# Block products of four recurrence heads in one PSUM bank and one run

## The chip, the cores and the metric

The kernel runs on one core of a Trainium2 chip. The metric is the device time of one execution in microseconds (us), the median of several runs. A core has TensorE (PE; its weight loads are listed apart as PEld), VectorE (DVE), ScalarE (ACT), GpSimd (POOL) and SyncE (SP, which issues most DMAs). The profile comes from one further execution, recorded by the hardware profiler.

## The reference

Two layers of a hybrid decoder trunk for 512 tokens of width 1024. Each layer normalises its input, projects it, runs two groups of heads, and projects back with a residual. What matters here is the recurrence group (8 heads with 128 x 128 states):

```python
def hgrn2(q, f_logit, i, lb):
    qf = jax.nn.silu(q.astype(jnp.float32))
    logf = jnp.logaddexp(jnp.log(jnp.maximum(lb, LB_FLOOR)),
                         jnp.log1p(-lb) + jax.nn.log_sigmoid(f_logit.astype(jnp.float32)))
    k = -jnp.expm1(logf)
    ...
        scores = jnp.einsum('bhtd,bhsd,bhtsd->bhts', qch, kch, decay)
        o = jnp.einsum('bhts,bhsv->bhtv', scores, vch)
        o = o + jnp.einsum('bhtd,bhdv->bhtv', qch * jnp.exp(b), state)
...
def hybrid_layer(x, w_in, w_out, g_pre, g_post, lb, g_head, sinks):
    h = rms_norm(x, g_pre)
    proj = jnp.einsum('bsd,de->bse', h, w_in)
    q_h, f_h, i_h, z_h, q_a, k_a, v_a, z_a = jnp.split(proj, SPLIT_POINTS, axis=-1)
    o_h = hgrn2(q_h, f_h, i_h, lb)
    o_h = rms_norm(o_h, g_head).reshape(B, S, HG_WIDTH).astype(z_h.dtype) * jax.nn.silu(z_h)
    ...
    y = jnp.einsum('bse,ed->bsd', jnp.concatenate([o_h, o_a], axis=-1), w_out)
    return x + rms_norm(y, g_post)
```

## The kernel before

**Projections.** Every weight piece (128 x 512) is loaded by DMA into a tile `raw`, split by ACT into a rounded part `whi` (L181) and by DVE into the rest `wlo` (L182), and multiplied in three products per piece with the two parts of the activations `hhi` and `hlo` (L293). One call of `step()` issues three such matmuls. Two units of output (tiles `pj`, three PSUM banks) are in work at a time. The pieces are converted by a plan that counts steps and stays ahead of their use.

**Streams.** Attention and recurrence are generators that issue their own instructions and then yield a weight. `merge` interleaves them with the projection steps in proportion to these weights. So the weights that a generator yields set how many projection matmuls stand between two pieces of its work on PE. Instructions under `pin` keep the order in which the code issues them; the others are placed by a scheduler.

**Recurrence.** A head's masked score matrix `A` (128 x 128 for each of four token blocks) is built by levels: pairs of neighbouring tokens first (the base blocks), then blocks of 2, 4, 8, 16, 32 and 64. `prepare(a)` makes, for heads a and a + 1, the operands of the base products in the buffers `qb` and `kb` (L706 to L710) and the operands of the first level in `q` and `k` (L713 and L714). `spread` then issues 16 base products of 32 x 32 for a head (L688), four beside each other in the array by `tile_position`. As fp32 matmuls they count twice in the profile: 32 instructions MATMUL and as many weight loads for each head. The result of a head fills one bank, in the diagonal blocks only, and `keep_spread` copies it under a mask into `A` (L692). `hgrn(a)` takes four heads, a group, through the six levels: the products of a level (L744 for the first four levels, L750, L755) go into two of the three banks `sc`, in turn; then `q` and `k` are scaled for the next level (L762 on DVE, L763 on POOL), and DVE copies the products into `A` under a mask (L772). After that come the states and outputs, which use the two banks `ac`.

**The order around the change.** The base products of a group come in two runs on PE: those of the first two heads at the end of `prepare`, in two `sc` banks, and those of the other two at the start of `hgrn`, in the two `ac` banks. The buffers `qb` and `kb` of all heads come from the pool tag `b`, which holds two pairs, so the second two heads' operands follow the first two heads' products. After the second run `hgrn` yields 1.5, which becomes nine projection matmuls, and then the first level's products start. With two groups to a layer and two layers there are four groups.

Of the kernel before, what the change touches and what calls it, by code (L numbers as in the profile page):

```python
# [20 lines left out]
NT = SEQ // 128  # L21
# [49 lines left out]
def hybrid_kernel(ctx: ExitStack, tc: tile.TileContext, x, wkv, win, wout, g_pre, g_post, lbp, ghead, sinks,  # L71
                  gcol_c, cos_f, sin_f, cos_t, sin_t, masks_c, out):
    nc = tc.nc
    P = 128
# [9 lines left out]
    def pin(ins):  # L84
        return tc.keep_in_program_order(ins)
# [8 lines left out]
    def sc():  # L94
        sc_turn[0] += 1
        return sc_tiles[sc_turn[0] % SC]

    def ac():
        ac_turn[0] += 1
        return ac_tiles[ac_turn[0] % len(ac_tiles)]  # L100

    def tmp(tag, dt=F32, n=1):

        t = tp.tile([P, n, 512] if n > 1 else [P, 512], dt, tag=tag, name=tag, bufs=TB[tag])
        return t
# [25 lines left out]
    for l in range(1, DEPTH):  # L131
        i = plan_order.index((l, "kv"))
# [224 lines left out]
    def halves(tag):  # L357
        t = tmp(tag, n=2)
        return [t[:, 0], t[:, 1]]
# [77 lines left out]
    def layer(l, last):  # L437
# [240 lines left out]

        on = {}

        As, kbs, qbs, tots, quad = {}, {}, {}, {}, {}

        def spread(j, bank):

            for n in range(NT):
                for b in range(4):
                    c = slice(n * P + 32 * b, n * P + 32 * b + 32)
                    pin(nc.tensor.matmul(bank[32 * b:32 * b + 32, c], lhsT=kbs[j][:, c], rhs=qbs[j][:, c], start=True, stop=True,  # L688
                                         tile_position=(0, 32 * b)))

        def keep_spread(j, bank):
            nc.vector.copy_predicated(As[j].rearrange("p (n t) -> p n t", n=NT), bmask.unsqueeze(1).broadcast_to([P, NT, P]),  # L692
                                      bank.rearrange("p (n t) -> p n t", n=NT))

        def prepare(a):

            t = tmp("a", n=2)
            nc.gpsimd.memset(t, 0.0)
            blocks = lambda t, w: t.rearrange("p (b j) -> p b j", j=w)
            for j in range(a, a + 2):  # L700
                As[j] = t[:, j - a]
                f, k, q = quad[j] = fT.pop(j), kT.pop(j), qT.pop(j)
                f2, k2, q2 = (blocks(t, 2) for t in (f, k, q))
                qb, kb = halves("b")
                qb2, kb2 = blocks(qb, 2), blocks(kb, 2)
                nc.vector.reciprocal(kb2[:, :, 1], f2[:, :, 1])  # L706
                nc.scalar.copy(qb2[:, :, 0], q2[:, :, 0])
                nc.vector.tensor_tensor(qb2[:, :, 1], q2[:, :, 1], f2[:, :, 1], op=ALU.mult)
                nc.scalar.copy(kb2[:, :, 0], k2[:, :, 0])
                nc.vector.tensor_tensor(kb2[:, :, 1], kb2[:, :, 1], k2[:, :, 1], op=ALU.mult)  # L710
                qbs[j], kbs[j] = qb, kb

                nc.gpsimd.tensor_tensor(k2[:, :, 0], k2[:, :, 0], f2[:, :, 1], op=ALU.mult)  # L713
                nc.vector.tensor_tensor(q2, qb2, f2[:, :, 0].unsqueeze(2).broadcast_to([P, SEQ // 2, 2]), op=ALU.mult)  # L714
                nc.vector.tensor_tensor(f2[:, :, 0], f2[:, :, 0], f2[:, :, 1], op=ALU.mult)
                tots[j] = f2[:, :, 0]
                yield 3.5
            if a % 4 == 0:
                banks = [sc(), sc()]
                for i in range(2):  # L720
                    spread(a + i, banks[i])
                for i in range(2):
                    keep_spread(a + i, banks[i])

        def hgrn(a):
            hs = [(j, *quad.pop(a + j)) for j in range(4)]
            banks = [ac(), ac()]
            for i in range(2):
                spread(a + 2 + i, banks[i])
            for i in range(2):  # L730
                keep_spread(a + 2 + i, banks[i])
            yield 1.5
            for hh in (2, 4, 8, 16, 32, 64):
                nb = SEQ // (2 * hh)
                per, qu = nb // NT, nb // NT // 4
                Ls = [sc(), sc()]
                for j, f, k, q in hs:
                    L, i = Ls[j // 2], j % 2
                    qv = q.rearrange("p (b two j) -> p b two j", two=2, j=hh)
                    if hh <= 16:  # L740
                        for n in range(NT):
                            for b in range(4):
                                o_, blk, c = n * P + 32 * b, n * per + b * qu, 256 * i + n * 64 + 16 * b
                                pin(nc.tensor.matmul(L[32 * b:32 * b + 32, c:c + 16], lhsT=k[:, o_:o_ + 32],  # L744
                                                     rhs=qv[:, blk:blk + qu, 1, :], start=True, stop=True, tile_position=(0, 32 * b)))
                    elif hh == 32:
                        for n in range(NT):
                            for b in range(2):
                                o_, r_, c = n * P + 64 * b, 64 * b + 32 * (n % 2), 64 * i + n // 2 * 32
                                pin(nc.tensor.matmul(L[r_:r_ + 32, c:c + 32], lhsT=k[:, o_:o_ + 32],  # L750
                                                     rhs=q[:, o_ + 32:o_ + 64], start=True, stop=True, tile_position=(0, r_)))
                    else:
                        for n in range(NT):
                            o_, b, c = n * P, n % 2, 128 * i + n // 2 * 64
                            pin(nc.tensor.matmul(L[64 * b:64 * b + 64, c:c + 64], lhsT=k[:, o_:o_ + 64],  # L755
                                                 rhs=q[:, o_ + 64:o_ + 128], start=True, stop=True))
                for two in (hs[:2], hs[2:]):
                    for j, f, k, q in two:
                        qv = q.rearrange("p (b two j) -> p b two j", two=2, j=hh)
                        kv_ = k.rearrange("p (b two j) -> p b two j", two=2, j=hh)  # L760
                        tv = tots[a + j].rearrange("p (b two) -> p b two", two=2)
                        nc.vector.tensor_tensor(qv[:, :, 1, :], qv[:, :, 1, :], tv[:, :, 0].unsqueeze(2).broadcast_to([P, nb, hh]), op=ALU.mult)  # L762
                        nc.gpsimd.tensor_tensor(kv_[:, :, 0, :], kv_[:, :, 0, :], tv[:, :, 1].unsqueeze(2).broadcast_to([P, nb, hh]), op=ALU.mult)  # L763
                        t2 = sm.tile([P, nb], F32, tag=f"tot{hh}", name=f"tot{hh}", bufs=4)
                        nc.vector.tensor_tensor(t2, tv[:, :, 0], tv[:, :, 1], op=ALU.mult)
                        tots[a + j] = t2
                    for j, f, k, q in two:
                        A, L, i = As[a + j], Ls[j // 2], j % 2
                        if hh <= 16:
                            Av = A.rearrange("p (n b two j) -> p n b two j", n=NT, two=2, j=hh)[:, :, :, 1, :]  # L770
                            mv = lmask[hh].rearrange("p (b j) -> p b j", j=hh).unsqueeze(1).broadcast_to([P, NT, per, hh])
                            nc.vector.copy_predicated(Av, mv, L[:, 256 * i:256 * i + 256].rearrange("p (n b j) -> p n b j", n=NT, j=hh))  # L772
                        elif hh == 32:
                            Av = A.rearrange("p (m two t) -> p m two t", m=NT // 2, two=2)
                            for b in range(2):
                                for e in range(2):
                                    nc.scalar.copy(Av[64 * b:64 * b + 32, :, e, 64 * b + 32:64 * b + 64],
                                                   L[64 * b + 32 * e:64 * b + 32 * e + 32, 64 * i:64 * i + 64].rearrange("p (m t) -> p m t", m=NT // 2))
                        else:
                            Av = A.rearrange("p (m b t) -> p m b t", m=NT // 2, b=2)  # L780
                            for b in range(2):
                                nc.scalar.copy(Av[0:64, :, b, 64:128],
                                               L[64 * b:64 * b + 64, 128 * i:128 * i + 128].rearrange("p (m t) -> p m t", m=NT // 2))
                    yield 3.0

            kps = []
            for j, f, k, q in hs:
# [230 lines left out]
    m, n = head[0], head[1]  # L1018
# [43 lines left out]
    amask, bmask = masks[:, 0:128], masks[:, 128:256]  # L1062
# [40 lines left out]
    for run in [layer(l, l == DEPTH - 1) for l in range(DEPTH)]:  # L1103
        run()
# [60 lines left out]
```

## Time and profile before

| What | Value |
|---|---|
| Device time, median of 3 runs | 922.8 us (922.64 to 923.39) |
| Profiled execution: its span, first to last instruction | 921.4 us |
| Mean granted TensorE clock in it | 0.998 |
| HBM read, written | 86.93 MB, 12.58 MB |
| First run of base products of the first group | starts at 195.50 us |
| Second run; first level's products | 207.32; 210.30 us |

The page gives for each engine its busy time, share of the span and count of instructions. The chain is followed back from the last instruction: at each step to what released it. A group's row has line, engine, operation, output and input tiles, shape and count, then its busy time and the mean of one in ns, and the idle time ahead of it with what ended most of it. A row of the time line has start, duration, engine, line, operation and tiles, and in brackets the idle time before it with its releaser; rows of equal kind that follow each other are merged, with their count. A table by window has for each engine the busy time and in brackets how many instructions ran in the window. "issue" is a wait for nothing that the profile shows.

### The profile page before, as it was taken

The page shows a single profiled execution, that of the slowest core. Times are in us where ns is not written, and L with a number is a line of the kernel's source. Part 1 is how long each engine was busy: PE and PEld are TensorE (multiplying, and loading weights), DVE is VectorE, ACT ScalarE, POOL GpSimd, SP SyncE. Part 2 cuts the span into 40 slices and gives each one's busy share as a digit, 9 for nine tenths or more (in the row PEclk, how much of TensorE's full clock was granted, in tenths as well). Part 3 has the DMA queues.
Part 4 walks back from the last instruction along what each step waited for, and adds up shares of the span by engine and source line. Part 5 has one row for each costly group of instructions (what it writes and reads, how often), then busy time and mean ns, then how long its engine had stood idle before and what let it go on. Part 6 is the DMA issues. An engine that isn't in the chain of part 4 may idle for free.

```text
span 921.4 us, 19000 instructions
## 1 busy us (share of the span) xinstructions
PE 904.5 (98%) x7240; PEld 752.0 (82%) x7240; DVE 667.3 (72%) x1326; ACT 463.4 (50%) x1100; POOL 272.9 (30%) x292
## 2 busy tenths in 40 slices
PE   8999999999999999999989999999999999999996
PEld 7888887888888888888878878888788888888885
DVE  5967977869854896655786689876889449866556
ACT  6535767652755423534463366686446463245242
POOL 3325443304313142121332254450134022330102
PEclk9999999999999999999999999999999999999999
DMA  6684612333221432334356556222322323213413
GB/s 224 192 231 136 172 36 81 92 93 94 70 85 54 130 91 70 92 106 129 111 164 177 161 147 173 58 69 92 94 70 81 96 77 94 82 47 94 136 35 137
DMA packets 56570, 100.74 MB, mean 109 GB/s; under 512 B 6560, under 2 KB 9120, under 8 KB 56480
## 3 DMA queue, kind: packets, MB, share of 16 engines
q1 hardware_dynamic: 56192, 99.40, 36.6%
q8 instruction: 57, 0.93, 0.4%
q14 instruction: 33, 0.27, 0.1%
q10 hardware_dynamic: 288, 0.14, 0.1%
HBM read 86.93 MB, written 12.58 MB: 108 GB/s over the span
## 4 chain that ended last, share of the span: by engine, by line
PE 88%; DVE 6%; ACT 3%; issue 1%; POOL 1%; DMA 0%; POOLq 0%; DVEq 0%; ACTq 0%
PE pj L293 72%; PE sc L561 2%; PE sc L744 2%; PE ac L614 2%; PE ac L815 2%; DVE wlo L182 1%; PE ac L818 1%; PE ac L802 1%; PE sc L588 1%; ACT s L575 1%; PE sc L867 1%; PE sc L790 1%; POOL r L354 1%; DVE a L943 1%; PE sc L550 0%
## 5 line engine op out<-in xcount | busy, mean ns | idle before, releaser
L182 DVE TENSOR_TENSOR wlo<-raw,whi 128x512 fp32r<-128x512 f32 x249 | 182.9, 748 | 50.0 <-ACT whi L181 49.3
L181 ACT CAST whi<-raw 128x512 fp32r<-128x512 f32 x256 | 154.2, 620 | 106.0 <-PE pj L293 95.2
L293 PE MATMUL pj<-hhi,wlo 128*128 128x512 f32 x512 | 203.8, 398 | 0.0
L293 PE MATMUL pj<-hhi,whi 128*128 128x512 f32 x512 | 199.8, 390 | 0.0
L293 PE MATMUL pj<-hlo,whi 128*128 128x512 f32 x512 | 199.6, 390 | 0.0
L293 PE MATMUL pj<-whi,ops 128*128 128x512 f32 (+1 forms) x520 | 172.5, 394 | 0.0
L293 PEld LDWEIGHTS pj<-hhi,whi 128*128 128x128 f32 x512 | 96.1, 188 | 20.7
L293 PEld LDWEIGHTS pj<-whi,ops 128*128 128x128 f32 x520 | 97.2, 188 | 19.3
L293 PEld LDWEIGHTS pj<-hhi,wlo 128*128 128x128 f32 x512 | 96.1, 188 | 19.3
L293 PEld LDWEIGHTS pj<-hlo,whi 128*128 128x128 f32 x512 | 96.3, 188 | 18.6
L293 PE MATMUL pj<-whi,hlo 128*128 128x512 f32 x256 | 103.6, 405 | 0.0
L293 PE MATMUL pj<-wlo,ops 128*128 128x512 f32 (+1 forms) x260 | 100.8, 388 | 0.0
L293 PE MATMUL pj<-wlo,hhi 128*128 128x512 f32 x256 | 100.5, 392 | 0.3 <-DVE wlo L182 0.2
L293 PE MATMUL pj<-whi,hhi 128*128 128x512 f32 x256 | 100.3, 392 | 0.0
L763 POOL TENSOR_TENSOR k<-k,tot 128x256 f32<-128x256 f32 x80 | 64.2, 831 | 107.2 <-PE sc L744 57.7
L575 ACT ACTIVATE s<-sc,negm 128x128 f32<-128x128 f32 x128 | 45.5, 368 | 38.9 <-DVE negm L569 34.8
L762 DVE TENSOR_TENSOR q<-q,tot 128x256 f32<-128x256 f32 x80 | 48.8, 647 | 12.8 <-PE sc L750 7.0
L293 PEld LDWEIGHTS pj<-whi,hhi 128*128 128x128 f32 x256 | 48.1, 188 | 10.3
L293 PEld LDWEIGHTS pj<-wlo,ops 128*128 128x128 f32 x260 | 49.0, 188 | 8.8
L293 PEld LDWEIGHTS pj<-wlo,hhi 128*128 128x128 f32 x256 | 48.3, 189 | 9.1 <-DVE wlo L182 1.2
L293 PEld LDWEIGHTS pj<-whi,hlo 128*128 128x128 f32 x256 | 48.2, 188 | 8.0
L582 POOL TENSOR_TENSOR s<-s,sums 128x512 f32<-128x512 f32 x32 | 34.1, 1067 | 44.5 <-DVE sums L580 29.2
(188 smaller groups left out, 1416.2 us busy)
## 6 DMA issues: line engine op xcount, KB each, us to landing
raw<-in_win_dram SPq DMA_DIRECT2D x192, 256.0 KB, 2.7
raw<-in_wout_dram SPq DMA_DIRECT2D x64, 256.0 KB, 2.7
stack<-rot SPq DMA_DIRECT2D x16, 512.0 KB, 3.4
qs<-stack SPq DMA_DIRECT2D x32, 256.0 KB, 4.9
a<-in_x_dram SPq DMA_DIRECT2D x12, 256.0 KB, 3.0
raw<-in_wkv_dram SPq DMA_DIRECT2D x8, 256.0 KB, 4.2
x_mid<-a SPq DMA_DIRECT2D x8, 256.0 KB, 2.1
a<-x_mid SPq DMA_DIRECT2D x8, 256.0 KB, 3.2
```

What stands on the lines that cost most here:

```text
L181: keep(nc.scalar.copy(hi, v))
L182: keep((nc.gpsimd if i in on_pool and i % 2 else nc.vector).tensor_tensor(lo, v, hi.bitcast(F32), op=ALU.subtract))
L293: nc.tensor.matmul(u.o, lhsT=u.sta(k, u.w)[i], rhs=u.mov(k, u.w)[j], start=(n == 0), stop=(n == len(u.list) - 1))
L354: keep(nc.gpsimd.tensor_tensor(r, t, mhalf[:, 0:1], op=ALU.pow))
L561: pin(nc.tensor.matmul(S[:, h * 256:(h + 1) * 256], lhsT=q[:, 2 * hp_ + h, t_], rhs=kst[v][p][:, (n - 1) * P:(n + 1) * P], start=(h == 0 a ...
L575: nc.scalar.activation(pt[:, h * P:(h + 1) * P], cur[h], AF.Exp, bias=negm[:, h:h + 1], scale=SCALE, accum_out=sums[:, h:h + 1])
L582: nc.gpsimd.tensor_tensor(pv, pv, sums.unsqueeze(2).broadcast_to([P, 4, P]), op=ALU.mult)
L614: pin(nc.tensor.matmul(U, lhsT=vst[v][:, blk, :], rhs=d, start=(i == 0), stop=(i == len(terms) - 1)))
L744: pin(nc.tensor.matmul(L[32 * b:32 * b + 32, c:c + 16], lhsT=k[:, o_:o_ + 32], rhs=qv[:, blk:blk + qu, 1, :], start=True, stop=True, tile_ ...
L762: nc.vector.tensor_tensor(qv[:, :, 1, :], qv[:, :, 1, :], tv[:, :, 0].unsqueeze(2).broadcast_to([P, nb, hh]), op=ALU.mult)
L763: nc.gpsimd.tensor_tensor(kv_[:, :, 0, :], kv_[:, :, 0, :], tv[:, :, 1].unsqueeze(2).broadcast_to([P, nb, hh]), op=ALU.mult)
L815: pin(nc.tensor.matmul(O[:, c], lhsT=A[:, c], rhs=vs(j, n), start=(n == 0), stop=False))
```

## The change

The base products of all four heads of a group go into one `sc` bank, each block in 32 columns of its own, at the start of `hgrn`, directly ahead of the first level's products. `keep_spread` makes two copies of two heads each, spreading a block's 32 columns over the four places of a row under the same mask, and stands behind the first level's products. The first two heads' `qb` and `kb` stay in tag `b`; those of the other two come from the tags `s` and `u`. The yield of 1.5 ahead of the first level is gone, and the first level yields 4.5 instead of 3.0.

```diff
-        As, kbs, qbs, tots, quad = {}, {}, {}, {}, {}
-
-        def spread(j, bank):
-
-            for n in range(NT):
-                for b in range(4):
-                    c = slice(n * P + 32 * b, n * P + 32 * b + 32)
-                    pin(nc.tensor.matmul(bank[32 * b:32 * b + 32, c], lhsT=kbs[j][:, c], rhs=qbs[j][:, c], start=True, stop=True,
-                                         tile_position=(0, 32 * b)))
-
-        def keep_spread(j, bank):
-            nc.vector.copy_predicated(As[j].rearrange("p (n t) -> p n t", n=NT), bmask.unsqueeze(1).broadcast_to([P, NT, P]),
-                                      bank.rearrange("p (n t) -> p n t", n=NT))
+        As, pairs, kbs, qbs, tots, quad = {}, {}, {}, {}, {}, {}
+
+        def spread(a, bank):
+
+            for j in range(4):
+                for n in range(NT):
+                    for b in range(4):
+                        c, o_ = slice(n * P + 32 * b, n * P + 32 * b + 32), P * j + 32 * n
+                        pin(nc.tensor.matmul(bank[32 * b:32 * b + 32, o_:o_ + 32], lhsT=kbs[a + j][:, c], rhs=qbs[a + j][:, c],
+                                             start=True, stop=True, tile_position=(0, 32 * b)))
+
+        def keep_spread(a, bank):
+            for i in range(2):
+                nc.vector.copy_predicated(pairs[a + 2 * i].rearrange("p j (n b t) -> p (j n) b t", n=NT, b=4),
+                                          bmask.rearrange("p (b t) -> p b t", b=4).unsqueeze(1).broadcast_to([P, 2 * NT, 4, 32]),
+                                          bank[:, 256 * i:256 * i + 256].rearrange("p (m t) -> p m t", t=32).unsqueeze(2)
+                                          .broadcast_to([P, 2 * NT, 4, 32]))
...
+            pairs[a] = t
...
-                qb, kb = halves("b")
+                qb, kb = halves("b") if a % 4 == 0 else (tmp("s"), tmp("s" if j == a else "u"))
...
-            if a % 4 == 0:
-                banks = [sc(), sc()]
-                for i in range(2):
-                    spread(a + i, banks[i])
-                for i in range(2):
-                    keep_spread(a + i, banks[i])
...
-            banks = [ac(), ac()]
-            for i in range(2):
-                spread(a + 2 + i, banks[i])
-            for i in range(2):
-                keep_spread(a + 2 + i, banks[i])
-            yield 1.5
+            bank = sc()
+            spread(a, bank)
...
+                if hh == 2:
+                    keep_spread(a, bank)
...
-                    yield 3.0
+                    yield 4.5 if hh == 2 else 3.0
```

What stands where on PE in the first group, before (48 projection matmuls stand between the first two pieces, nine between the last two; of these the ones next to the products are shown):

```order
L688 MATMUL sc_79<-b 32x32 x16
L688 MATMUL sc_80<-b 32x32 x16
L293 MATMUL pj<-hhi,wlo 128x512
...
L293 MATMUL pj<-hhi,whi 128x512
L688 MATMUL ac_82<-b 32x32 x16
L688 MATMUL ac_81<-b 32x32 x16
L293 MATMUL pj<-hhi,wlo 128x512
...
L744 MATMUL sc_78<-q,k 32x16 x32
L744 MATMUL sc_79<-q,k 32x16 x32
L293 MATMUL pj<-hhi,wlo 128x512
```

The same place on PE in the changed kernel, where L689 is the base products and L739 the first four levels (a row's count is of fp32 matmuls, two instructions MATMUL each):

```order
L293 MATMUL pj<-hhi,whi 128x512
L689 MATMUL sc_79<-b 32x32 x32
L689 MATMUL sc_79<-s 32x32 x16
L689 MATMUL sc_79<-s,u 32x32 x16
L739 MATMUL sc_80<-q,k 32x16 x32
L739 MATMUL sc_78<-q,k 32x16 x32
L293 MATMUL pj<-hhi,wlo 128x512
```

The first run has moved back to the second, and the first level has moved up to it; the next level's products follow after 51 projection matmuls, 33 before. The other three groups read alike. On DVE at the same place, in the kernel before:

```order
L692 COPY_PREDICATED a<-masks,ac_82 128x512
L692 COPY_PREDICATED a<-masks,ac_81 128x512
...
L762 TENSOR_TENSOR q<-q,f 128x128x2
L846 TENSOR_TENSOR z_2395<-z_2394,oa 128x512
L762 TENSOR_TENSOR q<-q,f 128x128x2
L772 COPY_PREDICATED a<-masks,sc_78 128x128x2 x2
L848 TENSOR_TENSOR ops<-z_2395,ops 128x512
L182 TENSOR_TENSOR wlo<-raw,whi 128x512
```

And in the changed kernel (L694 is the masked copy of the base blocks, L759 the scaling of `q`, L769 the masked copy of a level, L843 a step of the output gate):

```order
L694 COPY_PREDICATED a<-masks,sc_79 128x1024 x2
L759 TENSOR_TENSOR q<-q,f 128x128x2 x2
L769 COPY_PREDICATED a<-masks,sc_80 128x128x2 x2
L759 TENSOR_TENSOR q<-q,f 128x128x2 x2
L843 TENSOR_TENSOR z_2469<-z_2468,oa 128x512
L182 TENSOR_TENSOR wlo<-raw,whi 128x512
```

The copies of all four heads now stand together, directly ahead of the first level's scaling and of the next `wlo`.

## The prediction

> **What bounds the kernel now.** I read the page first, then PE's time line around the runs that the change touches, then who waited for whom.
>
> ```profile
> PE 904.5 (98%) x7240; PEld 752.0 (82%) x7240; DVE 667.3 (72%) x1326; ACT 463.4 (50%) x1100; POOL 272.9 (30%) x292
> PE 88%; DVE 6%; ACT 3%; issue 1%; POOL 1%; DMA 0%; POOLq 0%; DVEq 0%; ACTq 0%
> q8 instruction: 57, 0.93, 0.4%
> ```
>
> PE is busy 98% of the span and 88% of the chain that ends last. Every other engine has slack. So each microsecond in PE's stream, gained or lost, moves the end by about as much, and the work is to price that stream. The third row (a DMA queue with its packets, MB and share) is needed below.
>
> ```profile
> 193.15 0.39 PE L293 MATMUL pj<-hhi,whi 128*128 128x512 f32 x1
> ...
> 195.19 0.39 PE L293 MATMUL pj<-hhi,whi 128*128 128x512 f32 x1
> 195.50 0.76 PE L688 MATMUL sc<-b 128*32 128x32 f32 x64
> 196.20 0.50 PE L293 MATMUL pj<-hhi,wlo 128*128 128x512 f32 x1
> 196.53 0.40 PE L293 MATMUL pj<-hlo,whi 128*128 128x512 f32 x1
> 196.77 0.40 PE L293 MATMUL pj<-hhi,whi 128*128 128x512 f32 x1
> ...
> 209.98 0.40 PE L293 MATMUL pj<-hhi,whi 128*128 128x512 f32 x1
> 210.30 1.35 PE L744 MATMUL sc<-q,k 128*32 128x16 f32 x128
> 211.58 0.50 PE L293 MATMUL pj<-hhi,wlo 128*128 128x512 f32 x1
> 211.92 0.39 PE L293 MATMUL pj<-hlo,whi 128*128 128x512 f32 x1
> 212.15 0.39 PE L293 MATMUL pj<-hhi,whi 128*128 128x512 f32 x1
> ```
>
> **A run's price.** From 193.15 to 195.19 nine projection matmuls start, 0.227 us apart. Around the first run of block products (64 instructions of the kind MATMUL) three such steps take 196.77 - 195.19 = 1.58 us instead of 0.68, so the run costs 0.90. Around the first run of level-2 products (128 of them) they take 2.17, so that run costs 1.49. The difference, 0.59 for 64 more, is 9.2 ns for each small matmul with its weight load. What is left of 0.90 is 0.31 us that a run costs for being a run: the time to go from wide tiles to narrow ones and back.
>
> **What the change removes from PE.** Each group of four heads had two runs of 64 and one of 128, 0.90 + 0.90 + 1.49 = 3.29 us. Now it has one run of 256: 0.31 + 256 x 0.0092 = 2.67. That is 0.62 per group and **2.5 us** for the four groups (four heads, two groups to a layer). The products themselves are as many and as large as before.
>
> **What the change adds to PE.** The level-2 run does not cost the same in all four groups:
>
> ```profile
> 319.74 1.56 PE L744 MATMUL sc<-q,k 128*32 128x16 f32 x128
> 664.93 1.66 PE L744 MATMUL sc<-q,k 128*32 128x16 f32 x128
> 774.57 1.37 PE L744 MATMUL sc<-q,k 128*32 128x16 f32 x128
> 664.93 1.13 PEld L744 LDWEIGHTS sc<-q,k 128*32 128x32 f32 x115 [0.36 <-issue]
> 666.28 0.21 PEld L744 LDWEIGHTS sc<-q,k 128*32 128x32 f32 x13 [0.23 <-issue]
> 319.70:320.85 1.15, 1.15 (x110) 1.10 (x109) 1.15 (x4) 0.91 (x2) 0.54 (x1) 1.00 0.79 280
> 320.85:666.20 345.35, 340.19 (x2406) 283.37 (x2396) 255.04 (x508) 174.25 (x434) 103.87 (x104) 1.00 0.39 117
> ```
>
> Two take 1.35 and 1.37, the other two 0.21 and 0.31 longer. In the longest, PE's weight loads stop after 115 of 128 and go on at 666.28, and the wait is put down to "issue": no engine or transfer that the profile knows was late. In the other the stop comes after 109 loads, near 320.8. The last row (a table by window; its second count is of weight loads) gives the distance: 2,396 loads, as many matmuls, and 72 semaphore instructions in the records between make 4,864 instructions, which is 19 x 256 exactly. And 256 is a known size: the queue of kind "instruction" in the first fence moved 57 packets of 0.93 MB / 57 = 16.3 KB, and PE's 7,240 matmuls and 7,240 loads make 254 instructions for each. So PE's code comes in blocks of 256 instructions, and both stops stand where one block ends. I read them as PE having used up a block before the next was there.
>
> How long does a block take to come? From the stop at 666.28 I go back 256 instructions: 115 loads and 115 matmuls, one semaphore, the nine projection matmuls with their loads (18), which leaves 7 in the tail of the run before:
>
> ```profile
> 661.95 0.65 PEld L688 LDWEIGHTS ac<-b 128*32 128x32 f32 x64 [0.35 <-issue]
> ```
>
> Its last load starts near 662.5 (0.65 us less one load of 0.11), and the block that was missing came 3.8 us later. The same count in the other group ends 19 instructions before the end of its run, near 317.2, and PE goes on near 320.9: 3.7 us. So a block seems to be asked for when PE enters the one before it, and is there some 3.75 us after. In the stream of projections 256 instructions last 128 x 0.227 = 29 us, so nothing is seen of it. In a run of small matmuls 256 instructions last 128 x 9.2 ns = 1.18 us.
>
> The joint run is 256 matmuls and 256 loads, 512 instructions without a pause: two ends of blocks lie in it, 1.18 us apart, and none of the three old runs held more than one. Counting the rows of the changed order from the known ends, the first lies about 146, 239, 251 and 88 instructions into the four joint runs, so the second, 256 further, lies inside each of them (at 507 of 512 in the third, where a few semaphores more or less don't matter: the next projections would wait instead). At the second end PE waits 3.75 - 1.18 = 2.57 us, four times: **10.3 us**. The old stops, 0.21 + 0.31 = **0.5 us**, go, as they came from an old run and the next lying 18 instructions apart. The ends of this term: nothing if I misread the two stops, and 3.8 us a run if nothing of the transfer lies beside the burst, 15 in all. I take 2.57, since both stops give the same 3.75, and 2.0 to 3.2 as what transfers may vary by, an estimate from the spread of 0.1 between only two cases and a margin for it.
>
> **What else moves, and its cover.**
>
> ```profile
> 203.45 0.68 DVE L714 TENSOR_TENSOR q<-b,f 128x512 f32<-128x512 f32 x1
> 196.91 1.67 POOL L713 TENSOR_TENSOR k<-k,f 128x256 f32<-128x256 f32 x2 [27.47 <-ACT b L709]
> L692 DVE COPY_PREDICATED a<-masks,sc 128x512 f32<-128x512 uint8 x8 | 5.5, 745 | 5.7 <-PE sc L688 5.7
> L692 DVE COPY_PREDICATED a<-masks,ac 128x512 f32<-128x512 uint8 x8 | 5.4, 727 | 0.0
> L762 DVE TENSOR_TENSOR q<-q,f 128x256 f32<-128x256 f32 x16 | 9.1, 586 | 0.7 <-PE sc L744 0.7
> L772 DVE COPY_PREDICATED a<-masks,sc 128x256 f32<-128x256 uint8 x64 | 28.7, 509 | 0.0
> PE pj L293 <- DVE wlo L182: 0.2, 1, 0.2
> ```
>
> Level 2 now starts nine projection matmuls (2.0 us) earlier against its operands. The last of them were done at 204.1 on DVE and 198.6 on POOL; the joint run starts near 206.4 (the old run at 207.3 less the 0.9 of the run that left) and reaches level 2 1.2 us later. Cost nothing, 3 us of cover. Operands of heads 3 and 4 move to other buffers, so their preparation no longer waits until the first run has let go of the old ones: DVE and ACT start earlier, on engines that have slack; nothing.
>
> On DVE four masked copies of 512 columns (0.74 us) become two of 1,024. Their shape is not in the trace; by the rate of L692 each takes 1.46, by that of L772 (256 columns in 0.51, another strided form) 2.0, so a group takes 2.9 to 4.1 us instead of 2.9. I take 1.46. They now stand together right behind the joint run, ahead of the first level's multiplications. The next level's products write the bank that they read and one of the level-2 banks; ahead of that stand two copies (2.9), four multiplications (4 x 0.59) and two masked copies (2 x 0.51), 6.3 us, or 7.4 with slow copies, and PE comes there only 51 projection matmuls later, 11.6 us. Cost nothing, 4 us of cover or more. Behind the copies in DVE's queue stands also a wlo that PE needs. PE waited for one only once in the whole span, for 0.2 us (last row), so the 1.5 us by which it may move lie in its slack. I put nothing for it, and 1.5 us a group as the far end if that slack is gone. No DMA is issued at another place on purpose; the pieces' loads follow the same projection steps.
>
> **The sum**, against the profiled execution: span 921.4 - 2.5 - 0.5 + 10.3 = 928.7. The median of the runs is 1.4 above that span, so **930.1 us**, slower by 0.8%.
>
> **The rivals.**
> - No wait for code (13%): the two stops have another cause, or the next two blocks are kept ready. Then only the saving is left, 922.8 - 2.5 - 0.5 = 919.8 at best, 920.3 if the old stops stay: faster. For it: the 2.5 us rest on two runs measured directly, and the stops are only two. Against it: both stand at the same place of a block, and no engine was late. [...]
> - A shorter wait (10%): PE's sequencer reads ahead of the array, and where the first end lies early in the run it asks for the block while the projections still go slowly. If on average half the wait is hidden that way, 4 x 1.3 = 5.2 us: 921.4 - 3.0 + 5.2 + 1.4 = 925.0. For it speaks the fourth group (88 instructions in); against it, that in the two measured cases the read-ahead is in the 3.75 already.
> - The wait, and DVE's cover gone as well (6%): the delayed wlo costs its 1.5 us in each group, 930.1 + 6 = 936.
> - That the products do not come as one run at all is excluded by the order: no projection stands between them.
>
> **How the numbers follow.** The forecast has 71%: 2.0 to 3.2 us for each wait give 921.4 - 3.0 + 8.0 + 1.4 = 927.8 to 932.6. The range must hold 8 in 10, so it takes in the shorter wait: 924.0 to 933.5. Outside stay the first rival and the last, 19%. A measurement of this kernel can tell about 0.2% (1.8 us) from no change. Faster by more: the first rival, 0.13. Within: the shorter wait where most of it is hidden, 0.03. Slower: the rest, 0.84.
>
> **What would show it.** In the changed profile each joint run should be one group of 256 matmuls with a stop of 2 to 3 us among its weight loads, put down to "issue", with 256 instructions from the entry of the last block to it; PE's busy time should stay and its share fall. A run that goes through in 2.4 us gives it to the first rival. Masked copies near 1.46 us and no wait of PE at the next level's products would confirm the cover; a wait of PE for L694 or for a wlo right behind it would give the third rival its price. The prediction is wrong at its root if the stops were not waits for code.

## The result and the profile after

| | before | changed |
|---|---|---|
| median of the runs | 923.1 us (922.6 to 924.3) | 936.2 us (933.5 to 936.7) |
| profiled run, and its span | 922.8 us, 921.4 us | 933.5 us, 931.8 us |
| ratio, with its 95% interval | | 1.013 (1.0114 to 1.0146) |

The change makes the kernel 1.3% slower, and the time lies above the range that was given (924.0 to 933.5). The profiled run is the shortest of four; its mean granted clock is 0.992 and that of the others 0.990. What follows explains the profiled run; the others left no trace.

The page of the changed kernel, first the busy times, then the chain, then the queue that moves code:

```profile
PE 906.0 (97%) x7240; PEld 755.1 (81%) x7240; DVE 668.7 (72%) x1318; ACT 462.8 (50%) x1100; POOL 270.3 (29%) x292
PE 87%; DVE 7%; ACT 3%; issue 2%; POOL 1%; DMA 0%; POOLq 0%; DVEq 0%; SPq 0%; ACTq 0%
q8 instruction: 57, 0.93, 0.4%
```

PE is still what sets the end, with as many instructions. Its busy time grew by 1.5 us though runs were saved, and "issue" went from 1% to 2% of the chain. Who made PE wait (engine, line, releaser, then the sum, the number of waits and the longest):

```profile
PE sc L739 <- issue: 8.8, 4, 3.6
PE pj L293 <- DVE wlo L182: 0.2, 1, 0.2
```

Four waits of 8.8 us together stand in the first level's products, L739, and nothing that the profile knows was late there. The wait for a `wlo` is the same 0.2 us as before, and no wait for a masked copy is in the list. The joint runs on PE's time line (start, duration, instruction, count, and the idle time before it), the first part of the first run, then the stop in each of the four:

```profile
206.57 0.73 PE L689 MATMUL sc<-b 128*32 128x32 f32 x62
...
207.72 0.85 PE L739 MATMUL sc<-q,k 128*32 128x16 f32 x71
210.47 0.67 PE L739 MATMUL sc<-q,k 128*32 128x16 f32 x56 [1.90 <-issue]
...
323.15 0.40 PE L739 MATMUL sc<-q,k 128*32 128x16 f32 x10 [3.57 <-issue]
323.48 0.80 PE L293 MATMUL pj<-hhi,wlo 128*128 128x512 f32 x1
...
671.85 0.20 PE L739 MATMUL sc<-q,k 128*32 128x16 f32 x1 [1.64 <-issue]
...
781.76 0.93 PE L739 MATMUL sc<-q,k 128*32 128x16 f32 x82 [1.64 <-issue]
```

Each joint run stops once, with 56, 10, 1 and 82 of its 256 matmuls left. From one stop to the next the trace holds 2,560, 4,864 and 2,304 instructions of PE (matmuls, weight loads and semaphore instructions), each a multiple of 256: these are ends of blocks of code. The code queue agrees: during each stop, or up to 0.6 us ahead of it, one packet of 16,384 bytes starts on it (at 208.20, 320.82, 669.64 and 779.56), takes 0.93 to 0.96 us, and PE goes on 1.27 to 1.38 us after its end. One row shows something else: the first projection matmul behind the second stop (323.48) lasts 0.80 us, where 0.50 is usual. A table by window around that stop and the last one (window, its length, then for each engine busy time and count, the granted clock of TensorE, the DMA share and GB/s):

```profile
315.74:319.16 3.42, 3.42 (x230) 2.91 (x229) 0.61 (x1) 0.00 (x0) 0.27 (x1) 1.00 0.46 167
319.16:322.57 3.41, 0.43 (x44) 0.33 (x32) 3.41 (x6) 0.00 (x0) 2.18 (x3) 1.00 0.85 269
322.57:325.98 3.41, 2.83 (x16) 2.31 (x17) 0.77 (x3) 0.81 (x2) 0.84 (x1) 0.50 0.07 25
325.98:329.40 3.42, 3.42 (x10) 2.65 (x9) 3.41 (x7) 1.43 (x3) 0.00 (x0) 0.50 0.33 95
329.40:332.81 3.41, 3.41 (x16) 2.79 (x16) 0.89 (x2) 0.10 (x1) 0.00 (x0) 1.00 0.15 59
779.96:783.37 3.41, 1.77 (x101) 1.55 (x92) 3.41 (x4) 0.00 (x0) 2.00 (x3) 1.00 0.54 155
783.37:786.79 3.42, 3.42 (x9) 2.68 (x9) 3.42 (x7) 2.35 (x4) 1.71 (x2) 0.50 0.00 0
786.79:790.20 3.41, 3.41 (x16) 2.78 (x15) 2.54 (x6) 0.00 (x0) 0.00 (x0) 1.00 0.54 159
```

Behind the wait the granted clock is 0.50, for 6.83 us at the second stop and 3.41 us at the fourth, and PE looks fully busy while it gets through 9 or 10 projection matmuls where 16 would go. Half the busy time of these three stretches, (2.83 + 3.42 + 3.42) / 2 = 4.8 us, is lost to the clock. This is an estimate, and it more than covers PE's extra busy time.

**The account**: span before 921.4, less 2.5 for four joint runs and 0.5 for the old stops (both as predicted), plus 8.8 of waits and 4.8 of clock, is 932.0; the span is 931.8. It holds for this execution; the median of the runs lies 4.4 us above that span, where it lay 1.4 above it before.

### The profile page after: what moved, and what is told of

Same layout as the page of the kernel before. It is cut to its first block, busy times and chain, and to the rows that moved or that the text cites. A ratio compares the mean times of both kernels' runs of the same rounds, so it can differ in the third digit from the quotient of the medians.

```text
span 931.8 us, 18983 instructions
## 1 busy us (share of the span) xinstructions
PE 906.0 (97%) x7240; PEld 755.1 (81%) x7240; DVE 668.7 (72%) x1318; ACT 462.8 (50%) x1100; POOL 270.3 (29%) x292
## 4 chain that ended last, share of the span: by engine, by line
PE 87%; DVE 7%; ACT 3%; issue 2%; POOL 1%; DMA 0%; POOLq 0%; DVEq 0%; SPq 0%; ACTq 0%
PE pj L293 71%; PE sc L739 2%; PE sc L561 2%; PE ac L614 2%; PE ac L812 2%; DVE wlo L182 1%; PE ac L815 1%; PE ac L799 1%; PE sc L588 1%; ACT s L575 1%; PE sc L864 1%; POOL r L354 1%; PE sc L787 1%; PE sc L689 1%; DVE a L940 1%
## 5 line engine op out<-in xcount | busy, mean ns | idle before, releaser
L293 PE MATMUL pj<-hhi,wlo 128*128 128x512 f32 x512 | 205.0, 400 | 0.0
L293 PE MATMUL pj<-hhi,whi 128*128 128x512 f32 x512 | 201.3, 393 | 0.0
L293 PE MATMUL pj<-hlo,whi 128*128 128x512 f32 x512 | 201.2, 393 | 0.0
L293 PE MATMUL pj<-whi,ops 128*128 128x512 f32 (+1 forms) x520 | 171.9, 394 | 0.0
L293 PEld LDWEIGHTS pj<-hhi,whi 128*128 128x128 f32 x512 | 97.2, 190 | 20.9
L293 PEld LDWEIGHTS pj<-hlo,whi 128*128 128x128 f32 x512 | 97.4, 190 | 19.2
L293 PEld LDWEIGHTS pj<-hhi,wlo 128*128 128x128 f32 x512 | 97.1, 190 | 19.5
L293 PEld LDWEIGHTS pj<-whi,ops 128*128 128x128 f32 x520 | 97.3, 188 | 19.3
L760 POOL TENSOR_TENSOR k<-k,tot 128x256 f32<-128x256 f32 x80 | 62.0, 802 | 146.9 <-PE sc L739 96.4
L293 PE MATMUL pj<-whi,hlo 128*128 128x512 f32 x256 | 103.6, 405 | 0.0
L293 PE MATMUL pj<-wlo,ops 128*128 128x512 f32 (+1 forms) x260 | 100.7, 387 | 0.0
L293 PE MATMUL pj<-wlo,hhi 128*128 128x512 f32 x256 | 100.4, 392 | 0.3 <-DVE wlo L182 0.2
L293 PE MATMUL pj<-whi,hhi 128*128 128x512 f32 x256 | 100.3, 392 | 0.0
L759 DVE TENSOR_TENSOR q<-q,tot 128x256 f32<-128x256 f32 x80 | 54.1, 717 | 18.8 <-PE sc L739 9.7
L293 PEld LDWEIGHTS pj<-whi,hhi 128*128 128x128 f32 x256 | 48.1, 188 | 10.3
L293 PEld LDWEIGHTS pj<-wlo,ops 128*128 128x128 f32 x260 | 49.0, 188 | 8.8
L293 PEld LDWEIGHTS pj<-wlo,hhi 128*128 128x128 f32 x256 | 48.3, 189 | 8.9 <-DVE wlo L182 1.0
L293 PEld LDWEIGHTS pj<-whi,hlo 128*128 128x128 f32 x256 | 48.2, 188 | 8.1
```

What stands on the lines that cost most here:

```text
L293: nc.tensor.matmul(u.o, lhsT=u.sta(k, u.w)[i], rhs=u.mov(k, u.w)[j], start=(n == 0), stop=(n == len(u.list) - 1))
```

## The experiments

The theory after the result: PE waits at a block's end for code, and a wait can make the clock fall behind it. The rivals: the waits have to do with the operands, banks or copies of the joint run and not with its length; or the slow projection matmuls come from something else in the changed order, such as DVE's longer copies, and not from PE's having stood idle. The ratios are to the kernel before, taken along with them: its median was 923.6 us for the run broken up (both), the 32 tiny warm-up matmuls and the clock alone, and 923.4 for the other three.

**Breaking the run up.** The changed kernel with projection matmuls between the base products and the first level's products, nine or 18; the first level yields 3.0, as before the change; all else is as changed.

```diff
+            yield 1.5
...
-                    yield 4.5 if hh == 2 else 3.0
+                    yield 3.0
```

> The changed kernel with nine projection matmuls put back between the base products and the first level (a yield of 1.5 there, 3.0 after the first level); the single bank, the two wide masked copies and the new buffers stay. Theory A (PE waits for its code where two ends of blocks of 256 instructions lie in one burst, and the granted clock falls after such waits): the second end now comes some 3.4 us after the first, so a wait of 0 to 0.5 us a group is left and the clock stays near 0.998: 922 us (921 to 924). Rival B (the copies, the buffers or VectorE's queue cost the time): nothing of that is undone, so 933 us or more.

Measured: 923.4 us (922.7 to 924.5), ratio 0.9994 (0.9985 to 1.0003), span 921.4. One stop is left, and the clock does not fall:

```profile
319.27 1.20 PE L740 MATMUL sc<-q,k 128*32 128x16 f32 x109
321.58 0.36 PE L740 MATMUL sc<-q,k 128*32 128x16 f32 x19 [1.11 <-issue]
```

This is the time line of PE in the second group, where the end of a block still falls into the later run too soon behind the one before. The other has 18 between (`yield 3.0`):

> As the one before with eighteen projection matmuls between (yield 3.0). Theory A: over 5 us between the two ends of blocks, no wait for code, clock 0.998: the saving of one run a group (4 x 0.31) and of the old stops (0.5) is left, 921.1 us (920 to 922.5). Rival B: 933 us or more.

Measured: 921.7 us (921.0 to 922.2), ratio 0.9973 (0.9961 to 0.9984), span 919.4, mean clock 0.998. Its time line in the first group:

```profile
206.77 0.73 PE L689 MATMUL sc<-b 128*32 128x32 f32 x62
...
207.77 0.46 PE L689 MATMUL sc<-s,u 128*32 128x32 f32 x32
208.16 0.50 PE L293 MATMUL pj<-hhi,wlo 128*128 128x512 f32 x1
...
212.49 0.90 PE L740 MATMUL sc<-q,k 128*32 128x16 f32 x81
```

No stop is left, in any group, and it is faster than both kernels. Operands, banks and copies are those of the change, so they do not make the waits by themselves; the run has to be unbroken. It also prices the saving: two runs a group in place of three save 4 x 0.31 = 1.2, with the old stops 1.7, and the span fell by 2.0.

**Moving the block ends.** If the waits stand where blocks end, more instructions ahead must move them. The last warm-up matmul, at the program's start, becomes 32 tiny fp32 ones: the code behind lies 124 instructions further on.

```diff
-    pin(nc.tensor.matmul(warm, lhsT=ones[:, 0:P], rhs=ones, start=True, stop=True))
+    for _ in range(32):
+        pin(nc.tensor.matmul(warm[0:32, 0:32], lhsT=ones[:, 0:32], rhs=ones[:, 0:32], start=True, stop=True))
```

> The changed kernel, with nothing touched around the recurrence; the last warm-up matmul at the kernel's start (4 PE instructions) is replaced by 32 tiny ones (128), which shifts all later PE code by 124 instructions against its blocks. Theory A: in the first group the first end of a block comes to 22 instructions behind the burst's start, is passed by the sequencer while the projections still run slowly, and the stop of 2.1 us becomes under 0.5; in the other three the stops stay at 1.8 to 3.7 us, but stand 124 instructions earlier in the run (108 later in the fourth). Time 2 us below the changed kernel, 934 (931 to 936). Any theory without code blocks: all four stops stay where they are in the run, time as the changed kernel's, 936.

Measured: 933.5 us (932.5 to 934.2), ratio 1.0101 (1.0083 to 1.0119). PE's waits in it, and the first group's run:

```profile
PE sc L739 <- issue: 7.3, 3, 3.4
```

```profile
208.13 0.73 PE L689 MATMUL sc<-b 128*32 128x32 f32 x62
...
209.29 1.35 PE L739 MATMUL sc<-q,k 128*32 128x16 f32 x127
210.58 0.50 PE L293 MATMUL pj<-hhi,wlo 128*128 128x512 f32 x1
```

The first group's run goes through: its first block end now lies 21 instructions into the run. In the other three, at 114, 132 and 225, the waits stay, at the new ends:

```profile
320.94 0.83 PE L739 MATMUL sc<-q,k 128*32 128x16 f32 x72 [1.84 <-issue]
...
667.27 0.72 PE L739 MATMUL sc<-q,k 128*32 128x16 f32 x63 [2.04 <-issue]
...
781.55 0.42 PE L739 MATMUL sc<-q,k 128*32 128x16 f32 x17 [3.37 <-issue]
```

With 72, 63 and 17 matmuls left, where it was 10, 1 and 82, they have moved by about 124 instructions towards the start in the second and third group, and by 132 (256 - 124) towards the end in the fourth, where the expectation had counted 108. So the ends of blocks decide, and the end 21 instructions into a run cost nothing here. The clock falls twice, behind the waits of the third and fourth group.

In the next kernel tiny matmuls also stand behind groups 1 to 3 (23, 4 and 23), so that the first end lies 21 to 26 instructions into all four runs.

```diff
+PAD = {(0, 0): 23, (0, 4): 4, (1, 0): 23, (1, 4): 0}
...
+                for _ in range(PAD[l, a] if j == 3 else 0):
+                    pin(nc.tensor.matmul(O[0:32, 0:32], lhsT=A[:, 0:32], rhs=A[:, 0:32], start=True, stop=True))
```

> The kernel of the run named align, with 23, 4 and 23 tiny fp32 matmuls (4 PE instructions each, into a bank that is overwritten next) behind the first, second and third group, so that the first end of a block comes 21 to 25 instructions into each of the four joint runs. Order, engines, copies and buffers else as in the changed kernel: the bursts stay 512 instructions long. Theory A: the sequencer passes that end while projections still run, so the block for the second end is on its way in time; waits of 0 to 0.6 us at the second or third end, no stretch at half clock, clock 0.998, 922.5 us (921 to 925), though the 200 instructions added cost some 0.9 us. A rival that blames the burst itself, the copies or the buffers: 933 us or more.

Measured: 927.2 us (926.5 to 928.5), ratio 1.0041 (1.0026 to 1.0056), span 925.3. No wait is left in a joint run and the clock does not fall, as expected, but the time is above the expectation. PE's waits of this kernel, and its line of tiny matmuls by form:

```profile
PE pj L294 <- issue: 1.9, 3, 1.1
```

```profile
L812 PE MATMUL ac<-a 128*32 128x32 f32 x100 | 3.7, 197 | 0.0
```

Blocks end a third time some 20 instructions behind the run, and there PE waits 1.9 us in three groups, in the projections. The 100 added matmuls of L812 start, each with its weight load, about 34 ns apart (46 of them from 293.94 to 295.52), so they take 3.4 us, and the ones of the warm-up put off the first run by 0.9 (207.44 for 206.57). Then 918.4 + 1.9 + 3.4 + 0.9 = 924.6, which leaves 0.7 open. The padding eats what it saves.

**The clock alone.** The kernel before, with no joint run, in which PE is made to wait ahead of each group's first-level products: a tiny matmul, its copy on ACT, two multiplications on POOL, and a tiny matmul that needs them. The projection matmuls around it are pinned, so that none fills the wait.

```diff
+            pin(nc.tensor.matmul(Z[:, 0:4], lhsT=ident, rhs=ident[:, 0:4], start=True, stop=True))
+            pin(nc.scalar.copy(w[:, 0:4], Z[:, 0:4]))
+            for _ in range(2):
+                nc.gpsimd.tensor_tensor(w, w, w, op=ALU.mult)
+            pin(nc.tensor.matmul(Z[:, 8:12], lhsT=ident, rhs=w[:, 0:4], start=True, stop=True))
```

> The kernel before, where PE is made to wait in each group directly ahead of the first level's products: a tiny matmul, a copy on ScalarE, two multiplications on GpSimd of 1.1 us each and a tiny matmul that reads their result, with the projections held in order around it. No burst of 512 instructions is in it. If a wait of 2.5 to 3 us next to small products alone makes the granted clock fall: clock 0.990 to 0.994 with stretches at half clock behind some of the four waits, 935 to 940 us. If the fall needs the wait for code or the long burst: clock 0.998, 932 to 935 us (the waits alone).

Measured: 950.2 us (949.5 to 951.9), ratio 1.0282 (1.0264 to 1.0301), span 950.2. The waits came out longer than planned, 16.3 us in four, since the copy stood behind other work of ACT. The first of them in the table by window:

```profile
209.35:212.76 3.41, 2.26 (x11) 1.78 (x10) 2.83 (x13) 1.10 (x2) 0.00 (x0) 1.00 0.27 101
212.76:216.18 3.42, 0.00 (x0) 0.00 (x0) 1.38 (x3) 0.68 (x2) 2.46 (x2) 1.00 0.25 77
216.18:219.59 3.41, 3.30 (x132) 3.14 (x133) 2.08 (x4) 0.00 (x0) 2.62 (x4) 0.50 0.02 5
219.59:223.01 3.42, 3.42 (x9) 2.65 (x8) 3.42 (x6) 0.62 (x1) 1.83 (x3) 0.50 0.00 0
223.01:226.42 3.41, 3.41 (x16) 2.77 (x15) 0.42 (x1) 0.00 (x0) 0.00 (x0) 1.00 0.29 77
```

The clock falls to 0.50 for 6.83 us, and so behind each of the four waits. No joint run, no missing code, no longer copy is in this kernel: PE's idle time alone does it. In the eight stretches at half clock PE is busy for 25.07 us by the tables by window; half of it, 12.5, and 16.3 of waits make 921.4 + 28.8 = 950.2, the span. That it comes out so exactly is luck: half is a rough estimate, since the 128 small products of a level took 1.91 us at half clock and 1.35 at full.

**A shorter wait.** The same without the two multiplications on POOL.

```diff
-            for _ in range(2):
-                nc.gpsimd.tensor_tensor(w, w, w, op=ALU.mult)
```

> As the run named wait without the two GpSimd multiplications: the wait of PE ahead of the first level is now one copy on ScalarE behind what stands in its queue, 1.0 to 2.4 us. If the clock falls only where more than half of a 3.41 us stretch of its grid is idle (between 1.66 and 1.80 us in the runs so far): no fall behind waits under 1.6 us, one or two of the longer ones may bring one, clock 0.995 to 0.998, 929 to 934 us. If any wait ahead of small products does it: four falls, clock 0.990, 938 us or more.

Measured: 930.2 us (929.7 to 934.6), ratio 1.0082 (1.0059 to 1.0106), span 928.2. PE's waits, then the table by window at the first of them:

```profile
PE ac L742 <- ACT wt L741: 5.6, 4, 2.0
```

```profile
208.49:211.90 3.41, 2.31 (x11) 1.83 (x11) 2.83 (x13) 1.10 (x2) 0.00 (x0) 1.00 0.27 88
211.90:215.31 3.41, 2.50 (x134) 2.31 (x135) 3.10 (x6) 0.68 (x2) 2.05 (x3) 1.00 0.30 82
215.31:218.72 3.41, 3.41 (x17) 2.79 (x16) 3.41 (x6) 0.62 (x1) 2.29 (x3) 1.00 0.00 0
```

A wait of 2.01 us lies across two stretches here, 1.10 us of idle time in one and 0.91 in the other, and the clock stays at 1.00; the other three waits pass without a fall too. The waits give 5.6 of the 6.8 us by which the span grew. The longest of the four runs, 934.6 us, has a mean clock of 0.993 where the others have 0.998: by this figure the clock fell there, but that run left no trace.

**Once more.** The changed kernel unchanged, in the second session.

> The changed kernel once more, for a second profile of it beside the two below on one chip. Theory A: again four stops, each where 256 instructions from the entry of a block are used up, at the same counts as in the first profile (2496, 5056, 9920 and 12224 instructions from the first), 1.8 to 3.8 us each; stretches at half clock behind those stops that put more than half of a 3.41 us stretch of the clock's grid to idleness, wherever these fall. 936 us (933 to 938).

Measured: 935.0 us (934.5 to 936.8), ratio 1.013 (1.0113 to 1.0147), span 932.8. Waits at the same four ends of blocks, 10.1 us now, and again two falls of the clock, behind the second and the third stop (above, behind the second and the fourth). Its table by window at the first and the third stop:

```profile
206.21:209.63 3.42, 2.16 (x201) 1.98 (x200) 1.79 (x2) 0.00 (x0) 1.52 (x2) 1.00 0.43 145
209.63:213.04 3.41, 2.71 (x65) 2.35 (x66) 3.41 (x7) 0.00 (x0) 1.78 (x3) 1.00 0.03 5
...
667.01:670.43 3.42, 3.08 (x258) 2.59 (x256) 1.78 (x3) 0.00 (x0) 1.10 (x2) 1.00 0.54 158
670.43:673.84 3.41, 1.56 (x7) 1.29 (x8) 3.41 (x7) 0.00 (x0) 2.20 (x3) 1.00 0.02 5
673.84:677.25 3.41, 3.41 (x10) 2.63 (x9) 1.50 (x4) 1.56 (x3) 0.00 (x0) 0.50 0.00 0
```

Two waits that hardly differ, 1.96 and 2.18 us of idle time: the first is cut by the border of two stretches (1.26 and 0.70), and nothing falls; the third lies mostly in one (1.85), and the next stretch runs at half clock. So the place of a wait on this grid decides as well as its length. The account closes here too: half the busy time of the three stretches at half clock is 4.7 us, and 921.4 - 3.0 + 10.1 + 4.7 = 933.2, where the span is 932.8.

## Why the prediction was wrong

**The step that failed is the sum**: "921.4 - 2.5 - 0.5 + 10.3 = 928.7" counted the waits for code as idle time alone. It had no term for the granted clock, and no rival had one. The runs show what belongs there: behind a wait that left PE idle for 1.64 us or more of one stretch of 3.41 us, the granted clock was 0.50 for 3.41 or 6.83 us, and the projection matmuls started 0.43 us apart there (783.44 to 786.43 in the changed kernel), for 0.227 at full clock. That is 4.8 us in the profiled run, more than the 3.0 us saved by the change. With this term the account closes to 0.2 us (932.0 against 931.8).

Of the 6.1 us between forecast and median, 3.1 stand in the profiled span (931.8 for 928.7): 4.8 of clock, less 1.5 because the waits were shorter than forecast. The other 3.0 are the median's distance from that span, taken as 1.4 from the kernel before and 4.4 here. The other runs' clock of 0.990 for 0.992 makes about 1.9 of it, an estimate from rounded figures; the rest is open.

Step by step:

- **What bounds the kernel**: right. PE's share of the chain is 87%, 88% before, and what PE lost the span lost.
- **A run's price**: right. The one joint run that goes through in the kernel with the code moved gives it directly: the third projection matmul behind it starts at 211.14, the last ahead of it at 207.82, and 3.32 less three steps of 0.227 is 2.64 us, for 2.67 predicted. The run broken in two, without waits, brought 2.0 us where 1.7 follow from the same prices.
- **Blocks of 256 instructions, two ends in each joint run, a wait at the second**: right, and the four stops stand within 5 instructions of the counted places. The rival without a wait is refuted by the four stops. The two stops of the kernel before, on which the prediction rested, bear the same mark: packets of code from 318.26 to 319.48 and from 663.81 to 665.05, and PE going on at 320.85 and 666.28. Among projections PE crossed the ends of blocks unseen: no wait for "issue" stands in L293 in the changed kernel, where L739 has four of 8.8 us together.
- **The size of the wait**: 8.8 us in all for 10.3, each 1.64 to 3.57 for 2.57. From the entry of one block to the first instruction of the next pass 3.28, 4.96, 3.02 and 3.03 us in the trace, so the 3.75 that two cases gave was a fair mean with a far larger spread than the 0.1 between them. The spread lies in the start of the packet, 1.0, 2.6, 0.8 and 0.8 us after the entry; what follows it hardly varies.
- **The shorter wait**: its mechanism showed, but not where the prediction put it. A packet of code was seen to come up to 4.7 us ahead of a run (the last section has it), and in the kernels with the code moved an end 21 to 26 instructions into the run left no wait at the next end (0.0 us in five runs); one at 93, in the fourth group of the changed kernel, left 1.64 us.
- **DVE's copies and the `wlo`**: the cover held. The copies take 1.31 us on average (1.46 predicted), and PE waits for none. The time of 936 that this rival gave agrees with the measured median by chance: what it would have been made of did not happen.

```profile
L694 DVE COPY_PREDICATED a<-masks,sc 128x1024 f32<-128x1024 uint8 x8 | 10.1, 1313 | 9.2 <-PE sc L689 9.2
```

This is the group of the copies in the changed kernel; the 9.2 us of idle time ahead are DVE's, for PE, not the reverse.

## What to carry to other kernels

Count the instructions of a burst of small matmuls, weight loads included, against the blocks in which code arrives: here 256 in 1.2 us, while the next block takes 3 to 5 us. Put longer work into such a burst before a second end of a block falls into it; 18 projection matmuls between two halves made the change a gain of 0.3%. And price a wait of PE twice, as idle time and by the clock that it may cost behind it: here 8.8 us and 4.8, by the estimate above.

## What the runs showed of the hardware

- **The clock.** The falls begin and end on a grid of 3.41 us: in the changed kernel they last from 322.57 to 329.40 and from 783.37 to 786.79, and between the two starts lie 460.80 us, 135 x 3.413. By the busy times in the tables by window, stretches at full clock with up to 1.48 us of idle PE were followed by a full clock (1.48 from 317.17 to 320.58 in the kernel with the code moved, 1.36 from 206.52 to 209.93 in the changed one), and those with 1.64 us or more by half (1.64 from 779.96 to 783.37 and 2.98 from 319.16 to 322.57, both in the changed kernel); four of the profiled runs had such falls ahead of the end of the program (the changed kernel both times, the kernel with the code moved for the first group, and the one with 16.3 us of waits). (Counted from the last start of a matmul instead of from its modelled end, 1.48 and 1.64 become the 1.66 and 1.80 of the expectation above.) How long a fall lasts does not go by the idle time ahead: behind 2.98 us it lasted two stretches, behind 3.20 us (the kernel with the code moved, 777.97 to 781.38) one. In these cases it went with the projection matmuls that start in the first stretch at half clock: six behind the second stop of the changed kernel, where the fall lasted two stretches, eight behind the fourth, where it lasted one. Small products did not stand in for them: PE was busy for 3.30 us of such a stretch with 128 of them and the starts of two projection matmuls (216.18, above), and the fall lasted two. This is read off a few falls; no run was made to test it.
- **The read-ahead.** In the third joint run, which starts at 667.70 with a block's end at its first instruction, the next block was already on its way 4.7 us earlier; in the first, with the end 145 instructions in, it was moved only during the run. The DMA view of the changed kernel has one packet of the code queue in the window from 662.90 to 664.00 and none from there to 667.70; and none from 203.70 to 207.18, but one from there to 210.47, when PE went on. So code is asked for some tens of instructions ahead of the array, an estimate: 4.7 us are some 40 instructions of projections at 0.11 us each (half of 0.227). Of a burst, at 4.6 ns each (half of 9.2), 40 take 0.2 us, and PE waited.
- **The spread.** The same program waited 8.8 us for code in one execution and 10.1 in another, and its runs differ by 3.1 us where those of the kernel before differ by 1.7. Not tried was what makes a packet of code late. Other transfers alone do not order the cases: 259 GB/s ran in the 1.02 us between entry and packet at the first stop, 181 GB/s in the 2.64 us at the second.
